# A masked prefix sum over eight batches: one ring of seven places, with tables of addresses, in place of two halves of five

## The chip, the cores and the metric

The kernel runs on 1 core of one Trainium2 chip. The metric is the time of one execution on the device in microseconds. The kernel before takes 88.33 us (median of 3 runs, 87.98 to 88.53).

## The reference

```python
def setup_inputs():
    B, S, D = 8, 8192, 512
    return {
        "x": np.random.randn(B, S, D).astype(np.float32),
        "lengths": np.random.randint(16, S, size=(B,)).astype(np.int64),
        "w": np.random.randn(D, D).astype(np.float32),
    }

def reference(x, lengths, w):
    ...
    mask = (pos < lengths[:, None, None]).astype(np.float32)
    cs = np.cumsum(x * mask, axis=1)
    mid_features = cs[b_idx, (lengths // 2).clip(0), :]
    return np.matmul(mid_features[:, None, :], w).squeeze(1).astype(np.float32)
```

Of each batch only the sum of its first n rows is needed, n = min(length // 2 + 1, length); eight sums of 512 columns are then multiplied by w. So the work is to read n rows for each batch, and n is known only on the chip. The draw is the same each time: n = 570, 2690, 256, 2057, 905, 3772, 3859, 571. In blocks of 512 rows (1 MB) that is 1, 5, 0, 4, 1, 7, 7, 1 whole blocks, 26 together, and a remainder for each batch.

## The kernel before

SyncE brings the whole blocks, ScalarE the remainders, TensorE sums the rows by products with columns of ones and zeros, VectorE makes those columns. Batches go in pairs, and each batch of a pair has its own half of the buffer with five places:

```python
    NP = 5
    xt = sb("xt", [P, 2, NP, G, D])
    ...
    nc.sync.dma_start(            # block 0 of batch 0, before the lengths are known
        out=xt[:, 0, 0], in_=xf[:BLK].rearrange("(p g) d -> p g d", g=G)
    ).then_inc(s_full[0][0], 16)
    ...
    # SyncE: the lengths of a pair are loaded into registers; a block is issued when its place is free
                def load(k):
                    sp.dma_start(
                        out=xt[:, q, k % NP],
                        in_=rows(sp, at, base, k * BLK, BLK).rearrange("(p g) d -> p g d", g=G),
                    ).then_inc(s_full[q][k % NP], 16)
                def load_block(k):
                    sp.wait_ge(s_sum, until[q][k % NP])
                    ...
```

TensorE goes over the batches, and in each over two rounds of five blocks; nested compares end a round early:

```python
                with pe.Fori(0, B // 2):
                    for q in range(2):
                        keep_busy()               # two idle products
                        take(pe, s_cur[q], 1)
                        take(pe, s_rem[q], 16 * (len(PARTS) + 1))
                        for j in range(G):        # the remainder
                            mm = add(j, cur[:, q, B + j * B:2 * B + j * B], rem[:, q, j])
                            ...
                        def add_block(k):
                            if k:
                                keep_busy()
                            take(pe, s_full[q][k], 16)
                            for j in range(G):
                                mm = add(j, cur[:, q, :B], xt[:, q, k, j])
                            mm.then_inc(s_sum, 1)
                        with pe.Fori(0, -(-NB // NP)):
                            whole_blocks(pe, n, NP, add_block)
                            pe.reg_alu(n, n, NP * BLK, ALU.subtract)
                            pe.reg_alu(n, n, 0, ALU.max)
                    ...
                # the signal: its end tells VectorE that the sums are complete
                pe.matmul(idle_ps[:1, :1], lhsT=idle[:, :1], rhs=idle[:, :1], start=True,
                          stop=True).then_inc(s_pe, 1)
```

The last block of the last batch is set aside: it lands in a tile of its own (`last`, two halves), and is added behind the signal, so that the copies of the sums run beside it. After the signal come two copies, small products into `t_ps`, two transposes, 32 output products and the copies and writes of the output. This is called the tail below.

Of the kernel before, what the change touches and what calls it, by code (L numbers as in the profile page):

```python
# [8 lines left out]
I32 = mybir.dt.int32  # L9
BF16 = mybir.dt.bfloat16  # L10
# [6 lines left out]
def kernel(  # L17
# [19 lines left out]

    nc = tc.nc
# [4 lines left out]
    NB = S // 2 // BLK  # L43
    NP = 5
# [6 lines left out]
    WT = B + G * B  # L51
# [16 lines left out]
    xt = sb("xt", [P, 2, NP, G, D])  # L68
# [6 lines left out]
    cut = sb("cut", [1, 1])  # L75
    blk_i = sb("blk_i", [1, B + 1], I32)
    ones = sb("ones", [1, P])
    cnt = sb("cnt", [P, B], I32)
    cap = sb("cap", [P, B, G], I32)
# [6 lines left out]
    idle = sb("idle", [P, D], BF16)  # L86
    table = sb("table", [P, B * (WT + 1)])
    cur = sb("cur", [P, 2, WT])
    zero = sb("zero", [1, P])
# [11 lines left out]

    s_full = [[sem(f"full{q}_{k}") for k in range(NP)] for q in range(2)]
    s_rem = [sem(f"rem{q}") for q in range(2)]
    s_cur = [sem(f"cur{q}") for q in range(2)]
    s_last = [sem(f"last{h}") for h in range(2)]
    s_zero = [sem(f"zero{q}") for q in range(2)]
    s_w, s_len1, s_go, s_out = sem("w"), sem("len1"), sem("go"), sem("out")
    s_pool, s_dve, s_pe = sem("pool"), sem("dve"), sem("pe")
    s_act, s_sum = sem("act"), sem("sum")
# [5 lines left out]
    class Pairs:  # L115


        def __init__(self, eng, ready, count):

            self.eng = eng  # L120
            self.raw = [eng.alloc_register(f"n_{eng.engine.name}_{i}") for i in range(4)]
            self.t = eng.alloc_register(f"t_{eng.engine.name}")
            self.at = eng.alloc_register(f"pair_{eng.engine.name}")
            eng.reg_mov(self.at, 0)
            eng.wait_ge(ready, count)
            eng.load(self.raw, lens1[:, :4])

        def rows(self, q):

            n = self.raw[2 * q]  # L130
            self.eng.reg_alu(self.t, n, 1, ALU.logical_shift_right)
            self.eng.reg_alu(self.t, self.t, 1, ALU.add)
            self.eng.reg_alu(n, self.t, n, ALU.min)
            return n

        def step(self):

            alu, top = self.eng.reg_alu, 2 * B - 4
            alu(self.at, self.at, 4, ALU.add)
            alu(self.at, self.at, top, ALU.min)  # L140
            self.eng.load(self.raw, lens1[:, ds(self.eng.snap(self.at, min_val=0, max_val=top), 4)])

    def whole_blocks(eng, n, most, body, k=0):
        if k < most:
            with eng.If_cmp(n, BLK * (k + 1), "IS_GE"):
                body(k)
                whole_blocks(eng, n, most, body, k + 1)


    DVE_SEL, DVE_N, DVE_BLK, DVE_MASK = 1, 5, 10, 31  # L150
    DVE_LAST = DVE_MASK + 6
# [4 lines left out]
    nc.sync.dma_start(  # L156
        out=xt[:, 0, 0], in_=xf[:BLK].rearrange("(p g) d -> p g d", g=G)
    ).then_inc(s_full[0][0], 16)
# [8 lines left out]
    @block.sync  # L167
    def _(sp):
        alu = sp.reg_alu
        base, at = sp.alloc_register("sp_base"), sp.alloc_register("sp_at")  # L170
        sp.reg_mov(base, 0)

        items = sp.alloc_register("sp_items")
        sp.reg_mov(items, 1)
        until = [[sp.alloc_register(f"until{q}_{k}") for k in range(NP)] for q in range(2)]
        for u in until[0] + until[1]:
            sp.reg_mov(u, 1)
        has_last, last_at = sp.alloc_register("has_last"), sp.alloc_register("last_at")
        sp.reg_mov(has_last, 0)
        sp.reg_mov(last_at, 0)  # L180

        least = sp.alloc_register("sp_least")
        sp.reg_mov(least, BLK)
        ns = Pairs(sp, s_len1, 16)
        sp.sem_inc(s_go, 1)
        with sp.Fori(0, B // 2):
            for q in range(2):
                n = ns.rows(q)
                alu(items, items, 1, ALU.add)
                if q == 0:  # L190
                    alu(n, n, least, ALU.max)
                    sp.reg_mov(least, 0)
                else:
                    with sp.If_cmp(ns.at, 2 * B - 4, "IS_GE"):
                        alu(has_last, n, 9, ALU.logical_shift_right)
                        alu(has_last, has_last, 1, ALU.min)
                        alu(last_at, has_last, 9, ALU.logical_shift_left)
                        alu(n, n, last_at, ALU.subtract)
                        alu(last_at, n, ~(BLK - 1), ALU.bitwise_and)
                        alu(last_at, last_at, base, ALU.add)  # L200

                def load(k):
                    sp.dma_start(
                        out=xt[:, q, k % NP],
                        in_=rows(sp, at, base, k * BLK, BLK).rearrange("(p g) d -> p g d", g=G),
                    ).then_inc(s_full[q][k % NP], 16)

                def load_block(k):
                    sp.wait_ge(s_sum, until[q][k % NP])
                    alu(items, items, 1, ALU.add)  # L210
                    sp.reg_mov(until[q][k % NP], items)
                    if (q, k) == (0, 0):

                        with sp.If_cmp(ns.at, 1, "IS_GE"):
                            load(k)
                    else:
                        load(k)

                whole_blocks(sp, n, NB, load_block)
                alu(base, base, S, ALU.add)  # L220
            ns.step()

        with sp.If_cmp(has_last, 1, "IS_GE"):
            from_rows = rows(sp, at, last_at, 0, BLK).rearrange("(p g) d -> p g d", g=G)
            for h in range(2):
                sp.dma_start(
                    out=last[:, 2 * h:2 * h + 2], in_=from_rows[:, 2 * h:2 * h + 2]
                ).then_inc(s_last[h], 16)
        sp.wait_ge(s_dve, DVE_LAST)
        sp.dma_start(out=out[:, :D // 2], in_=o_sb[0][:]).then_inc(s_out, 16)  # L230

    @block.scalar
    def _(act):
        alu = act.reg_alu
        base, at = act.alloc_register("act_base"), act.alloc_register("act_at")
        act.reg_mov(base, 0)
        items = act.alloc_register("act_items")
        act.reg_mov(items, 1)
        until = [act.alloc_register(f"until_rem{q}") for q in range(2)]
        for u in until:  # L240
            act.reg_mov(u, 1)
        least = act.alloc_register("act_least")
        act.reg_mov(least, 1)
        act.memzero(rem[:, 0]).then_inc(s_zero[0], 1)  # L244
        ns = Pairs(act, s_go, 1)
        t = ns.t
        with act.Fori(0, B // 2):
            for q in range(2):
                n = ns.rows(q)
                act.wait_ge(s_zero[q], 1)  # L250
                act.wait_ge(s_sum, until[q])
                alu(items, items, 1, ALU.add)
                alu(until[q], items, 1, ALU.max)
                alu(t, n, 9, ALU.logical_shift_right)
                if q == 0:
                    alu(t, t, least, ALU.max)
                    act.reg_mov(least, 0)
                alu(items, items, t, ALU.add)
# [32 lines left out]
            ns.step()  # L291

        act.wait_ge(s_pe, B + 5)
# [6 lines left out]
    @block.gpsimd  # L300
    def _(pool):
        pool.sem_inc(s_sum, 1)
        pool.iota(pid[:], pattern=[[0, 1]], base=0, channel_multiplier=1)
        pool.iota(thr_i[:], pattern=[[P, 2]], base=0, channel_multiplier=1)
        pool.iota(fold_i[:], pattern=[[-1, B]], base=128, channel_multiplier=1).then_inc(s_pool, 1)
        pool.memset(idle[:], 1.0).then_inc(s_pool, 1)
        pool.wait_ge(s_dve, DVE_BLK)
        pool.memset(rem[:, 1], 0.0).then_inc(s_zero[1], 1)  # L308

    @block.vector  # L310
    def _(dve):
        done = 0

        def step(do, *args, **kw):

            nonlocal done
            if done:
# [3 lines left out]

        step(dve.memset, zero[:], 0.0)
        assert done == DVE_SEL
        step(dve.memset, ones[:], 1.0)
# [6 lines left out]
        step(dve.tensor_copy, out=blk_i[:, :B], in_=n_f[:])  # L331
        step(dve.tensor_scalar, out=blk_i[:, :1], in0=n_f[:, :1], scalar1=BLK, scalar2=None, op0=ALU.max)
        step(dve.tensor_scalar, out=cut[:], in0=n_f[:, B - 1:], scalar1=BLK, scalar2=None, op0=ALU.is_ge)
        step(dve.tensor_copy, out=blk_i[:, B:], in_=cut[:])
        step(dve.scalar_tensor_tensor, out=blk_i[:, B - 1:B], in0=cut[:], scalar=float(-BLK),
             in1=n_f[:, B - 1:], op0=ALU.mult, op1=ALU.add)
# [36 lines left out]
        for b in range(B):  # L373
            if b == 0:
                dve.wait_ge(s_dve, done)
            if b >= 2:
                dve.wait_ge(s_pe, b + 1)
# [137 lines left out]
```

## Time and profile before

| | before |
|---|---|
| median, runs | 88.33 us, 3 runs |
| profiled run, its span | 88.74 us, 86.9 us |
| moved | 31.28 MB |
| first product of the last ring block ("the pickup") | 77.43 us |
| signal | 79.86 us |
| end of the last copy | 84.05 us |

The span is split by the last three rows: up to the pickup the kernel reads rows, from the pickup to the signal it finishes the sums, and behind the signal is the tail. Two stretches of reading matter, and the tail. The columns are: stretch, length, busy time and number of instructions of PE, PEld, DVE, ACT, POOL, then the clock of TensorE, the busy share of the DMA engines, and GB/s.

```profile
10.00:14.00 4.00, 0.18 (x4) 0.15 (x8) 0.00 (x0) 0.00 (x0) 0.00 (x0) 1.00 1.02 418
22.00:28.00 6.00, 6.00 (x44) 0.92 (x40) 0.00 (x0) 0.00 (x0) 0.00 (x0) 1.00 0.95 325
79.86:84.05 4.19, 3.01 (x77) 1.84 (x73) 1.91 (x6) 0.52 (x2) 0.00 (x0) 1.00 0.00 0
```

At 22 to 28 us there is the hole, (422 - 325) x 6 = 580 KB or 1.4 us of full rate; the tail takes 4.19 us, all of it at full clock.

### The profile page before, as it was taken

What the parts mean: (1) busy time and instruction counts of PE and PEld (TensorE: products, weight loads), DVE (VectorE), ACT (ScalarE), POOL (GpSimd) and SP (SyncE); (2) the same over time, 40 slices, a digit from 0 to 9 for tenths busy, and PEclk for the clock granted to TensorE, in tenths of its full rate; (3) what the DMA queues carried; (4) which work ended last, traced back from release to release, by engine and by line L of the source; (5) the groups of instructions that cost most, each with busy time, mean ns of one, the idle gap of its engine ahead of it and who ended that gap; (6) DMA issues with size and microseconds to landing.
All of it is one profiled execution on the core that took longest, in us unless ns stands there. A gap on an engine that the chain in (4) does not pass through costs nothing. (4 is left out here: it accounts for less than half of the span.)

```text
span 86.9 us, 1465 instructions
## 1 busy us (share of the span) xinstructions
PE 57.1 (66%) x391; PEld 10.9 (13%) x391; DVE 8.2 (9%) x45; ACT 3.7 (4%) x5; POOL 2.8 (3%) x9
## 2 busy tenths in 40 slices
PE   0912206999999998089967197655956774559730
PEld 0400001011111211002101001010110110103420
DVE  1776000000000100000000000000000000001420
ACT  2920000000000000000000000000000000000020
POOL 4340000000000000000000000000000000000000
PEclk9999999999999999957999956999999999999999
DMA  2799999999999999999999999999999999991000
GB/s 30 313 411 422 417 421 422 419 426 422 317 338 345 407 422 426 431 404 417 427 419 426 415 419 422 422 422 422 422 422 422 422 419 422 409 387 60 0 0 8
DMA packets 4837, 31.28 MB, mean 360 GB/s; under 512 B 674, under 2 KB 690, under 8 KB 1218
## 3 DMA queue, kind: packets, MB, share of 16 engines
q1 hardware_dynamic: 3906, 27.27, 76.5%
q10 hardware_dynamic: 928, 3.97, 11.9%
q8 instruction: 1, 0.02, 0.1%
q14 instruction: 2, 0.02, 0.0%
HBM read 31.23 MB, written 0.02 MB: 360 GB/s over the span
## 5 line engine op out<-in xcount | busy, mean ns | idle before, releaser
L395 PE MATMUL s_ps<-xt,cur 128*8 128x512 f32 x200 | 28.7, 647 | 15.3 <-PEq L113 15.2
L402 PE MATMUL idle_ps<-idle 128*128 128x512 bf16 x50 | 16.8, 422 | 3.6 <-DVE table L319 3.5
L395 PE MATMUL s_ps<-rem,cur 128*8 128x512 f32 x64 | 9.8, 688 | 4.7 <-PEq L113 4.7
L395 PEld LDWEIGHTS s_ps<-xt,cur 128*8 128x8 f32 x200 | 4.0, 90 | 30.5 <-issue 30.4
L378 DVE COPY cur<-table 128x40 f32<-128x40 f32 x8 | 1.4, 184 | 53.4 <-PE s_ps L395 53.4
L402 PEld LDWEIGHTS idle_ps<-idle 128*128 128x128 bf16 x50 | 2.9, 99 | 26.8 <-issue 26.8
L295 ACT COPY o_sb<-o_ps 8x128 f32<-8x128 f32 x2 | 0.5, 258 | 78.6 <-PE o_ps L477 78.6
L413 PE MATMUL s_ps<-zero 1*128 1x512 f32 x2 | 2.1, 1131 | 2.3 <-DVE n_i L319 2.3
L319 DVE COPY s_sb<-s_ps 128x256 f32<-128x256 f32 x2 | 0.8, 424 | 17.3 <-PE idle_ps L450 17.3
L395 PEld LDWEIGHTS s_ps<-rem,cur 128*8 128x8 f32 x64 | 1.0, 88 | 9.3 <-issue 9.3
L244 ACT ACTIVATE rem<-rem 128x2048 uint32<-128x2048 uint32 x1 | 1.9, 1910 | 0.0
L308 POOL MEMSET rem<- 128x2048 f32 x1 | 1.8, 1805 | 1.7 <-DVE blk_i L319 1.7
L477 PE MATMUL o_ps<-wt,t_sb 128*8 128x128 f32 x32 | 1.1, 273 | 0.4 <-DVE t_sb L319 0.4
L244 ACT ACT_TABLE_LOAD x1 | 1.3, 1283 | 1.5 <-PEq L499 1.5
L406 PE MATMUL t_ps<-last,cur 128*8 128x128 f32 x32 | 1.3, 272 | 0.0
L477 PEld LDWEIGHTS o_ps<-wt,t_sb 128*8 128x8 f32 x32 | 0.8, 89 | 0.7 <-issue 0.7
L406 PE MATMUL t_ps<-s_sb,fold 128*8 128x128 f32 x8 | 0.8, 274 | 0.1
L416 PEld LDWEIGHTS n_ps<-n_f,ones 1*128 1x128 f32 x2 | 0.7, 332 | 1.0 <-DVE cut L319 0.5
L413 PEld LDWEIGHTS s_ps<-zero 1*128 1x128 f32 x2 | 0.5, 304 | 2.3 <-DVE n_i L319 2.3
L406 PEld LDWEIGHTS t_ps<-last,cur 128*8 128x8 f32 x32 | 0.8, 88 | 0.1
L319 DVE COPY o_sb<-o_ps 8x128 f32<-8x128 f32 x2 | 0.6, 281 | 1.0 <-PE o_ps L477 1.0
L319 DVE STREAM_TRANSPOSE t_sb<-t_ps 128x64 f32<-128x64 f32 x2 | 0.5, 250 | 1.0 <-PE t_ps L406 0.9
(43 smaller groups left out, 7.1 us busy)
## 6 DMA issues: line engine op xcount, KB each, us to landing
xt<-in_x_dram SPq DMA_DIRECT2D x25, 1024.0 KB, 12.7
rem<-in_x_dram ACTq DMA_DIRECT2D x3, 512.0 KB, 7.0
wt<-in_w_dram ACTq DMA_DIRECT2D x1, 1024.0 KB, 6.5
last<-in_x_dram SPq DMA_DIRECT2D x2, 512.0 KB, 10.2
rem<-in_x_dram ACTq DMA_DIRECT2D x3, 256.0 KB, 6.3
rem<-in_x_dram ACTq DMA_DIRECT2D x3, 128.0 KB, 7.1
rem<-in_x_dram ACTq DMA_DIRECT2D x3, 32.0 KB, 5.8
rem<-in_x_dram ACTq DMA_DIRECT2D x1, 64.0 KB, 6.1
```

The lines of the kernel that those rows point to most:

```text
L244: act.memzero(rem[:, 0]).then_inc(s_zero[0], 1)
L295: copy = act.copy(out=o_sb[1][:, j * P:(j + 1) * P], in_=o_ps[64 + 32 * j:64 + 32 * j + B, :P])
L308: pool.memset(rem[:, 1], 0.0).then_inc(s_zero[1], 1)
L319: do(*args, **kw).then_inc(s_dve, 1)
L378: dve.tensor_copy(out=cur[:, b % 2], in_=table[:, b * WT:(b + 1) * WT]).then_inc(s_cur[b % 2], 1)
L395: return pe.matmul(s_ps[32 * j:32 * j + B], lhsT=weights, rhs=rows, start=False, stop=False, skip_group_check=True, tile_position=(0, 32 * j))
L402: pe.matmul(idle_ps[:], lhsT=idle[:, :P], rhs=idle[:], start=True, stop=True)
L406: return pe.matmul(t_ps[32 * j:32 * j + B, :P], lhsT=weights, rhs=row[:, P * j:P * (j + 1)], start=False, stop=False, skip_group_check=Tru ...
L413: pe.matmul(s_ps[:], lhsT=zero[:], rhs=zero[:, :1].to_broadcast((1, D)), start=True, stop=False, skip_group_check=True)
L416: pe.matmul(n_ps[:, :B], lhsT=ones[:], rhs=n_f[:], start=True, stop=True).then_inc(s_pe, 1)
L477: mm = pe.matmul(o_ps[32 * j:32 * j + B, :P], lhsT=t_sb[:, kc, :B], rhs=wt[:, kc, j * P:(j + 1) * P], start=(kc == 0), stop=(kc == KC - 1) ...
```

## The change

The intent: the hole at 22 us comes from a buffer split by batch, where a long batch fills its half while the other half stands empty. One ring of seven places serves the blocks of all batches in order. For that each engine has to know which batch and which rows the i-th block of the ring is. VectorE works that out at the start: a table of the first row of every ring item (`addr`) and a table of the weight columns of every item (`wtab`). SyncE loads seven addresses at a time into registers; VectorE copies each item's weights into its place's columns when the place is freed, and then hands the place to SyncE. The first blocks of batches 0 and 1 are fetched blind, with known addresses, before anything is computed. SyncE, VectorE and TensorE walk a fixed number of rounds of seven items: ceil(63 / 7) = 9, enough for the longest lengths that can be drawn. The remainders are added by pairs in the first four rounds. Cut to its core:

```diff
-    NP = 5
+    BLIND = 2
+    NS = 7
+    ROUNDS = -(-(B * S // 2 // BLK - 1) // NS)
+    ITEMS = ROUNDS * NS
-    xt = sb("xt", [P, 2, NP, G, D])
+    xt = sb("xt", [P, NS, G, D])
+    def nested(eng, n, most, body, k=0):
         if k < most:
-            with eng.If_cmp(n, BLK * (k + 1), "IS_GE"):
+            with eng.If_cmp(n, k + 1, "IS_GE"):
                 body(k)
-                whole_blocks(eng, n, most, body, k + 1)
+                nested(eng, n, most, body, k + 1)
+    def less(eng, n, by):
+        eng.reg_alu(n, n, by, ALU.subtract)
+        eng.reg_alu(n, n, 0, ALU.max)
+    for b in range(BLIND):
+        nc.sync.dma_start(
+            out=xt[:, b], in_=xf[b * S:b * S + BLK].rearrange("(p g) d -> p g d", g=G)
+        ).then_inc(s_full[b], 16)
 # SyncE
+        sp.wait_ge(s_dve, DVE_ADDR)
+        sp.load(facts, meta[:])
+        sp.reg_mov(left, facts[0])
+        with sp.Fori(0, ROUNDS):
+            sp.load(at, addr[:, ds(sp.snap(off, min_val=0, max_val=ITEMS - NS), NS)])
+            def load(k):
+                take(sp, s_free[k], 1)
+                sp.dma_start(
+                    out=xt[:, k], in_=xf[ds(sp.snap(at[k]), BLK)].rearrange("(p g) d -> p g d", g=G)
+                ).then_inc(s_full[k], 16)
+            ...
+            nested(sp, left, NS, load_item)
+            less(sp, left, NS)
+            ...
+        with sp.If_cmp(facts[1], 1, "IS_GE"):     # the block set aside
+            ...
 # GpSimd
-        pool.wait_ge(s_dve, DVE_BLK)
-        pool.memset(rem[:, 1], 0.0).then_inc(s_zero[1], 1)
+        pool.wait_ge(s_dve, DVE_N)
+        pool.memset(rem[:, 1], 0.0).then_inc(s_rfree[1], 1)
 # VectorE: ... tables, 28 steps to the first addresses (DVE_ADDR), 51 to TensorE's start (DVE_MASK)
+        step(dve.tensor_scalar, out=blocks[:], in0=cnt[:], scalar1=9, scalar2=None,
+             op0=ALU.logical_shift_right)
+        ...
+        with dve.Fori(1, ROUNDS):
+            less(dve, left, NS)
+            ...
+            def weights(k):
+                take(dve, s_done[k], 1)
+                dve.tensor_copy(out=cur[:, k], in_=wtab[...]).then_inc(s_free[k], 1)
+            nested(dve, left, NS, weights)
 # TensorE
+        with pe.Fori(0, ROUNDS):
+            with pe.If_cmp(rest_rounds, 1, "IS_GE"):
+                for q in range(2):
+                    take(pe, s_rem[q], 16 * (len(PARTS) + 1))
+                    ...
+            def add_item(k):
+                keep_busy()
+                take(pe, s_full[k], 16)
+                for j in range(G):
+                    mm = add(j, cur[:, k], xt[:, k, j])
+                mm.then_inc(s_done[k], 1)
+            nested(pe, left, NS, add_item)
+            less(pe, left, NS)
+            less(pe, rest_rounds, 1)
+        tell()                                    # the signal
```

## The prediction

> **What bounds the kernel now.** I read the page's slices first, then the chain that ended last, then stretches of the span with their transfer rates, then the issues of transfers and the tensor engine's register work.
>
> ```profile
> PEclk9999999999999999957999956999999999999999
> DMA  2799999999999999999999999999999999991000
> GB/s 30 313 411 422 417 421 422 419 426 422 317 338 345 407 422 426 431 404 417 427 419 426 415 419 422 422 422 422 422 422 422 422 419 422 409 387 60 0 0 8
> PE 5%; DVE 2%; issue 0%
> ```
>
> From slice 3 to slice 35 the DMA engines move some 420 GB/s with every engine busy. 31.28 MB at that rate is 74 us of an 86.9 us span, so the kernel is bound by reading the rows, and the chain that ended last, 7% of the span, is only the tail behind the last rows. The one hole in the middle is slices 10 to 13. The same in stretches (columns: stretch, length, busy time and count of PE, PEld, DVE, ACT, POOL, then the PE clock, DMA share, GB/s):
>
> ```profile
> 16.00:22.00 6.00, 6.00 (x36) 0.74 (x28) 0.18 (x1) 0.00 (x0) 0.00 (x0) 1.00 1.01 422
> 22.00:23.00 1.00, 1.00 (x10) 0.23 (x10) 0.00 (x0) 0.00 (x0) 0.00 (x0) 1.00 0.92 262
> 23.00:25.00 2.00, 2.00 (x18) 0.23 (x10) 0.00 (x0) 0.00 (x0) 0.00 (x0) 1.00 0.96 365
> 25.00:28.00 3.00, 3.00 (x24) 0.46 (x20) 0.00 (x0) 0.00 (x0) 0.00 (x0) 1.00 0.94 320
> 34.00:76.00 42.00, 27.71 (x171) 4.13 (x170) 0.55 (x3) 0.00 (x0) 0.00 (x0) 0.92 1.01 421
> ```
>
> Against 422 GB/s the hole lost 160 x 1 + 57 x 2 + 102 x 3 = 580 KB, or 1.4 us. Its cause stands in the time line of SyncE's issues:
>
> ```profile
> 4.73 4.70 SPq L203 DMA_DIRECT2D xt<-in_x_dram  x5
> 21.12 45.52 SPq L203 DMA_DIRECT2D xt<-in_x_dram  x19
> ```
>
> Nothing is issued between 9.4 and 21.1 us: batch 1 fills all five places of its half (this draw's whole blocks per batch are 1, 5, 0, 4, 1, 7, 7, 1), and the next batch that has any uses the same half. TensorE starts only at 13.8, when the first remainder has landed, so a place comes free just as the queue runs dry at 22.
>
> [...]
>
> ```profile
> 33.17:36.58 3.41, 1.29 (x10) 0.11 (x2) 0.00 (x0) 0.00 (x0) 0.00 (x0) 1.00 1.00 423
> 36.58:39.99 3.41, 2.76 (x10) 0.28 (x10) 0.00 (x0) 0.00 (x0) 0.00 (x0) 0.50 1.01 408
> 46.83:50.24 3.41, 1.11 (x14) 0.24 (x10) 0.00 (x0) 0.00 (x0) 0.00 (x0) 1.00 1.01 418
> 50.24:53.65 3.41, 2.81 (x18) 0.28 (x10) 0.00 (x0) 0.00 (x0) 0.00 (x0) 0.50 1.04 425
> ```
>
> A stretch of 3.41 us with 1.1 to 1.3 us of matmuls is followed by one at clock 0.50; one with 2.1 us is not. [...] The trace of TensorE's sequencer differs: 64 to 72 ns where the program falls through, 200 to 220 ns where it jumps; I use those. [...] in the chain of table steps one 1x8 or 128x8 operation follows another every 0.19 us, a small memset every 0.13.
>
> **The change part by part.**
>
> *Places.* Seven places for all batches in place of two halves of five. After the two blind blocks SyncE can issue five more, so seven blocks (one more than now) are queued before any place must come free. The first place comes free at about the same time: TensorE now needs the remainders of batches 0 and 1 first (the second lands at 16.1 now; perhaps 14.5, its queue being shorter), 3.8 us of cold matmuls for both, then 1.0 for the idle pair and 1.0 for block 0, so about 20.5, plus VectorE's copy and the issue: 21.0. But with 1 MB more queued (2.5 us at 422 GB/s) the queue runs dry at 24.5 to 25 rather than 22. The new block is there in time, and TensorE then frees one every 1.5 us while one lands every 2.5. I expect most of the hole to close: **-1.2 us**.
>
> *Tables.* SyncE's first computed issue waits for 28 VectorE steps. Eight memsets from 1.0 to 2.3 us, three steps on the lengths to 2.9, four memsets, the broadcast of counts through TensorE until about 3.8, then thirteen steps of 0.19: 6.3 us. Two register loads (0.5 us for one here now) and some branches: first issue at 8.5 to 9, against 4.73 now. Three MB (weights, two blind blocks) plus the first remainders keep the engines busy until 10.5 to 12, since now the third such MB lands at 12.4. With about 1.2 us from issue to first packet (a reading of the first transfers), 10 us is just in time. The other 23 steps to TensorE's start end at about 11.8, before the remainders land. **0 us**, at worst +1.
>
> *Steady state.* Same bytes, same transfers of 1 MB; one 128x8 copy and one more hand-over per block on VectorE, hidden behind a depth of six blocks. **0 us**.
>
> *The end.* Here is what I think decides. The chain, and the register work at the end of the last two batches (TensorE's sequencer):
>
> ```profile
> 77.43 1.04 PE s_ps L395 x8
> 78.47 0.54 PE idle_ps L402 x2
> 79.01 0.97 PE s_ps L395 x8
> 79.98 0.10 PE idle_ps L450
> L145 PEldq COMPARE_BRANCH  x2: 201/206/210, 78.4 to 79.0; - x2
> L444 PEldq FUSED_REGOPS  x2: 53/53/53, 78.7 to 79.3; - x2
> L442 PEldq COMPARE_BRANCH  x2: 69/138/207, 78.8 to 79.4; - x2
> ```
>
> Now the last block is picked up at 77.3 and the signal matmul (L450), which releases the tail, starts at 79.86: 2.55 us for its four products, an idle pair and the last remainder. In the new kernel that remainder comes earlier, but the loop has ceil(63/7) = 9 rounds whatever the lengths are. This draw has 25 items in the ring (26 whole blocks, the last set aside): 3 full rounds, one of four, and **five empty rounds**, which TensorE's sequencer walks through after the last block, ahead of the signal. The rows show an empty turn of the present inner loop: 78.4, 78.7, 78.8, and again at 79.0, so a jumped compare costs 0.26, the register work 0.11, the jump back 0.26. An empty round has two jumped compares (remainders, items), one register group of four operations (0.15) and the jump back: 0.53 + 0.15 + 0.26 = 0.94. From pickup: 0.15 to the first compare, 0.68 for the rest of the fourth round, 5 x 0.94 less the 0.13 that the last saves = 4.57. Sum 5.4 us against 2.55: **+2.85 us**. The set-aside block lands at 78.6 and 79.8 now and hides none of it.
>
> *The clock.* Of these 5.4 us the matmuls fill 1, so a gap of over 4 us opens. [...] part of the tail (signal, 24 small products, 32 output products: 0.16 + 0.85 + 1.1 us warm, twice that cold) runs at half clock. At most +2, half of it on average: **+1.0 us**.
>
> Sum: 88.33 - 1.2 + 0 + 2.85 + 1.0 = **91.0 us**.
>
> **Rivals.** (A) *The intended gain.* The empty rounds cost little (the sequencer runs ahead of the matmuls), the hole closes, and the last remainder's 1.5 us leave the tail: then the set-aside block bounds the tail, which ends about 1.2 us earlier, plus 1.3 from the hole: 86. For it: at 77.5 the next compare does start while the products still run. Against it: they run 1 us, and the walk takes five. (B) *A new hole at the start.* The tables come late, the queue runs dry at 10 us and restarts with slow first packets, like now at 22: up to +1 to +1.5, so 92 to 92.5. For it: 28 steps and two loads are worked out with a margin of only a microsecond. Against: the remainders fill in. (C) *The hole stays*, since PE waits for two remainders and three hand-overs: 92.2. The rate stays low for 3 us after issues resumed, which speaks for it a little. (D) *The clock stays up* in the tail: 90.
>
> **Range and chances.** The main terms are the walk (2.85 +- 0.7), the clock (0 to 2), the hole (-1.4 to 0) and the start (0 to 1). Together some +-1.9 us for 8 in 10: 89.0 to 92.7. Two per cent up is 90.1; the sum lies 0.9 above it. Faster by over 2% (below 86.6) needs rival A whole: 0.04. Within 2%: 0.28. Slower: 0.68.
>
> **What would show it.** In the new profile: the rate at 20 to 30 us near 420 (hole closed) and the last block picked up at about 76; SyncE's first computed issue at 8.5 to 9 with no dip at 9 to 13; five repeats of two compares at TensorE's sequencer, 0.9 us each, between the last block and the signal matmul, which starts over 5 us after the pickup; a clock record of 0.50 in the tail; VectorE's wait for the signal in the chain. The prediction is wrong if the signal comes within 3 us of the pickup, or if the rate at the start drops.

## The result

The changed kernel takes **93.35 us** (median of 4 runs, 92.72 to 93.50), the kernel before 88.43 us (4 runs, 87.98 to 89.27) beside it. The ratio is 1.053 (95% interval 1.044 to 1.063): slower. A ratio, here and below, is the mean time of one kernel's runs over that of the other's (in the experiments without the profiled run), so not quite the ratio of the medians that are quoted. Executions over 1.5% slower than the fastest of the same kernel are left out of the means.

In the changed kernel's page, the slices of clock and rate and the shares of the chain that ended last:

```profile
PEclk9999999999999999999999999999999999997597
GB/s 29 340 416 426 369 288 413 437 419 416 434 408 423 416 423 430 415 395 426 412 423 430 416 416 430 408 426 416 419 423 426 419 419 407 177 2 0 0 0 7
PE 5%; issue 5%; DVE 1%
```

The hole in slices 10 to 13 (counted from 0) is gone. A dip has appeared in slices 4 and 5. The last transfer of rows lands just before 80 us in both kernels, but a longer stretch without any follows here, the clock falls to half in a part of it (its record is 0.50 from 82.9 to 86.3 us), and "issue" (time in which the engine waits for nothing that the profile shows), which had 0% of the chain, has 5%. The same stretches as before, with the tail last (signal to last copy):

```profile
10.00:14.00 4.00, 0.00 (x0) 0.00 (x0) 3.56 (x11) 0.00 (x0) 0.00 (x0) 1.00 0.90 314
11.00:12.00 1.00, 0.00 (x0) 0.00 (x0) 0.98 (x1) 0.00 (x0) 0.00 (x0) 1.00 0.76 115
22.00:28.00 6.00, 5.84 (x43) 0.92 (x40) 0.68 (x4) 0.00 (x0) 0.00 (x0) 1.00 1.01 418
82.83:87.77 4.94, 3.83 (x73) 2.67 (x73) 1.91 (x6) 0.52 (x2) 0.00 (x0) 0.65 0.00 0
```

At 22 to 28 us the rate rose from 325 to 418, which is what the ring was made for. At 10 to 14 us it fell from 418 to 314, a loss of 416 KB or 1.0 us, most of it in one microsecond. The tail ran at a mean clock of 0.65. The end of the chain, in order of time (start, duration, engine, tile, line, count):

```profile
77.61 1.05 PE s_ps L430 x8
78.65 4.18 issue
82.83 0.16 PE idle_ps L447
82.99 2.45 PE t_ps L436 x40
```

and what TensorE's sequencer did in the 4.18 us of "issue" (columns: line, operation, count, shortest, median and longest in ns, then the time of the first and of the last):

```profile
L136 PEldq COMPARE_BRANCH  x6: 201/201/207, 77.7 to 82.3; - x6
L461 PEldq COMPARE_BRANCH  x5: 201/201/201, 78.3 to 82.0; - x5
L141 PEldq FUSED_REGOPS  x6: 78/78/78, 77.9 to 82.5; - x6
```

L136 is the compare "is there a block k", L461 "are there remainders", L141 the two `less`. The first compare is the one that ends the fourth round; then the sequencer goes round five times with nothing to do, 0.92 us each ((82.3 - 77.7) / 5), and only then issues the signal (L447). Where the 3.8 us between the two spans (86.9 and 90.7 us) are:

| stretch | before | after | difference |
|---|---|---|---|
| start to pickup of the last ring block | 77.43 | 77.61 | +0.2 |
| pickup to signal | 2.43 | 5.22 | +2.8 |
| signal to end of the last copy | 4.19 | 4.94 | +0.75 |

So reading gained nothing, though its hole is closed; the walk through empty rounds stands between the last data and the signal; and the tail behind it runs partly at half clock.

### The profile page after: what moved, and what is told of

The parts are those of the page before. It is cut to its first block, busy times and chain, and to the rows that moved or that the text cites. A ratio compares the mean times of both kernels' runs of the same rounds, so it can differ in the third digit from the quotient of the medians.

```text
span 90.7 us, 1568 instructions
## 1 busy us (share of the span) xinstructions
PE 53.3 (59%) x387; PEld 11.6 (13%) x391; DVE 17.5 (19%) x86; ACT 3.7 (4%) x5; POOL 3.0 (3%) x11
## 5 line engine op out<-in xcount | busy, mean ns | idle before, releaser
L430 PE MATMUL s_ps<-xt,cur 128*8 128x512 f32 x200 | 26.1, 593 | 16.5 <-PEq L131 16.4
L430 PE MATMUL s_ps<-rem,cur_rem 128*8 128x512 f32 x64 | 9.3, 707 | 9.1 <-PEq L131 9.1
L443 PE MATMUL idle_ps<-idle 128*128 128x512 bf16 x46 | 14.2, 384 | 0.6 <-issue 0.6
L404 DVE COPY cur<-wtab 128x8 f32 x18 | 3.1, 171 | 36.3 <-DVEq L131 36.3
L430 PEld LDWEIGHTS s_ps<-rem,cur_rem 128*8 128x8 f32 x64 | 1.8, 95 | 15.8 <-issue 15.7
L447 PE MATMUL idle_ps<-idle 128*1 128x1 bf16 x1 | 0.2, 163 | 4.2 <-issue 4.2
L436 PE MATMUL t_ps<-last,e_last 128*8 128x128 f32 x32 | 2.3, 414 | 0.0
L397 DVE COPY cur_rem<-table 128x32 f32 x6 | 1.1, 182 | 5.8 <-DVEq L131 5.8
L436 PEld LDWEIGHTS t_ps<-last,e_last 128*8 128x8 f32 x32 | 1.3, 121 | 0.2
L289 DVE TENSOR_TENSOR wtab<-since 128x504 f32<-128x504 f32 x1 | 1.1, 1066 | 0.0
L289 DVE TENSOR_TENSOR part_a<-since,step_a 1x49 f32<-1x49 f32 (+1 forms) x2 | 1.1, 529 | 0.1
```

Of the source, the lines that this page charges most:

```text
L289: do(*args, **kw).then_inc(s_dve, 1)
L397: dve.tensor_copy(out=cur_rem[:, q], in_=rests[:, ds(dve.snap(at, min_val=1, max_val=B // 2 - 1), 1), q].rearrange("p o w -> p (o w)"),).t ...
L404: dve.tensor_copy(out=cur[:, k], in_=wtab[:, ds(dve.snap(at, min_val=1, max_val=ROUNDS - 1), 1), k].rearrange("p o b -> p (o b)"),).then_i ...
L430: return pe.matmul(s_ps[32 * j:32 * j + B], lhsT=weights, rhs=rows, start=False, stop=False, skip_group_check=True, tile_position=(0, 32 * j))
L436: return pe.matmul(t_ps[32 * j:32 * j + B, :P], lhsT=weights, rhs=row[:, P * j:P * (j + 1)], start=False, stop=False, skip_group_check=Tru ...
L443: pe.matmul(idle_ps[:], lhsT=idle[:, :P], rhs=idle[:], start=True, stop=True)
```

## The experiments

The theory after reading the two traces had four parts, each with a rival:

- *Walk*: the empty rounds of TensorE's loop hold the signal back. Rival: the signal waits for something else (a block, VectorE's own rounds), and cutting rounds moves nothing.
- *Clock*: the half clock from 82.9 us comes from that wait ("cold" is half clock here and below, "warm" is full clock), and the tail, 4.94 us in place of 4.19, pays for it. Rival: the slower tail comes from the new kernel's tail itself.
- *Start*: late tables open the new hole at 11 us, which takes back what the ring gains. Rival: the ring gained nothing, and both holes are hidden by the total of bytes.
- *Places*: the seventh place is what closes the hole at 22 us. Rival: the common ring alone does it, or the blind blocks.

Ten kernels ran, in three calls, each with runs of the kernel before on the same chip. In the second call (from e5 to e8) the runs of the kernel before are the first call's, made some ten minutes earlier, and one new one. The changed kernel itself wasn't run again beside the experiments.

### Four rounds only (e1_four_rounds)

TensorE walks only the rounds that this draw needs. The result is right for this draw only.

```diff
-        with pe.Fori(0, ROUNDS):
+        with pe.Fori(0, 4):
```

> TensorE's loop has 4 rounds in place of 9: right for this draw alone, whose 25 items fill 4. Theory (the walk through five empty rounds is 4.6 us of the loss, and the idle gap it makes costs 0.7 to 1.9 us more in the tail through the half clock): the signal matmul starts about 1.2 us after the last block is picked up (5.3 now), the tail runs at full clock, and the set-aside block, landing at about 80.0 us of the span, now bounds the tail. Time 87.7 +- 0.5 us, that is 5 to 6 us under the changed kernel and about 0.99 of the kernel before. Rival (the loss sits in the start or the transfers, and the walk hides behind the set-aside block): 92 us or more.

Measured: 88.19 us (87.61 to 88.79, 4 runs), ratio to before 0.9997 (0.990 to 1.009). The chain's end:

```profile
77.57 1.04 PE s_ps L430 x8
78.61 0.07 PE idle_ps L447
```

The signal comes 1.04 us behind the pickup in place of 5.22, and the tail behind it (78.61 to 82.76, 4.15 us) is warm again. The five empty rounds and their cold tail are therefore the whole of the loss, and VectorE's and SyncE's own empty rounds, which are still there, cost nothing that this kernel's chain shows. The set-aside block, which was expected to bound the tail, doesn't stand in the chain. What is left is ring, tables and weights together: the same time as before within about 1%. In the profiled runs this kernel's span was 1.2 us below before's, but two of its four runs were 0.6 to 0.9 us longer than the profiled one, and there is no trace of those.

### Warm walk (e2_warm_walk)

The empty rounds stay, but each has an idle pair in it, so that only the clock changes.

```diff
                     mm.then_inc(s_rdone[q], 1)
+            with pe.Else():
+                keep_busy()
```

> The walk stays, but in each empty round TensorE gets one idle pair (0.5 us of matmuls per 0.91 us round). Theory (part of the loss is the half clock that the idle gap brings): signal still 5.3 us (up to 5.6) after the pickup of the last block; no clock record of 0.50 in the tail; from the signal to the last copy 4.2 us as in the kernel before, in place of 4.9 in the profiled run. Time 92.1 us (91.7 to 92.6), 1.0 to 1.5 below the changed kernel, its runs at a mean clock near 1. Rival (the clock costs nothing): unchanged, 93.3.

Measured: 91.47 us (91.33 to 92.42, 4 runs), ratio 1.039 (1.029 to 1.049). The first idle pair of the walk and the signal, in the chain that ended last:

```profile
78.00 0.60 PE idle_ps L443 x2
...
82.47 0.12 PE idle_ps L447
```

The pickup is at 76.80, so the signal comes 5.7 us behind it (the idle pairs add 0.5), and the tail takes 4.06 us (82.47 to 86.53), all at full clock. So the slower tail was the clock's. The time lies a little below the expected range. Against the changed kernel it is 1.4% or 1.3 us by the ratios, whose intervals overlap a little, and 1.9 us by the medians, of different rounds. In this profiled run the pickup was 0.8 us earlier too, which the edit doesn't explain (start and tables are unchanged), so the clock's share can't be told from it better than "around 1 us".

### Known rows (e3_known_rows)

SyncE issues the five ring blocks behind the blind ones at once, with this draw's row numbers written in, and doesn't wait for the tables in round 0 (round 0 of its loop then issues nothing; that part of the edit isn't shown). Right for this draw only.

```diff
+        known = [S + k * BLK for k in (1, 2, 3, 4)] + [3 * S]
+        for k, row in zip(range(BLIND, NS), known):
+            take(sp, s_free[k], 1)
+            sp.dma_start(
+                out=xt[:, k], in_=xf[row:row + BLK].rearrange("(p g) d -> p g d", g=G)
+            ).then_inc(s_full[k], 16)
         sp.wait_ge(s_dve, DVE_ADDR)
```

> SyncE issues the first five blocks of the ring at once, with this draw's rows written into the program (wrong for other draws), so nothing at the start waits for the tables; the rest is as in the changed kernel. Theory (the late tables cost a hole at 11 to 13 us that ate most of what the ring won): the rate at 10 to 14 us stays near 420 GB/s, the last block is picked up 0.7 to 1.0 us earlier (76.5 to 76.9), time 92.4 (92.0 to 92.8). Rival (the engine that is furthest behind sets the last landing, and it lost less than the mean in that hole): a gain of 0.3 or less, 93.0 to 93.4. Second rival (more early blocks delay the remainders' landing and with it TensorE's start, so that the hole comes back at 22 to 28): no gain.

Measured: 92.20 us (92.05 to 92.41, 4 runs), ratio 1.044 (1.036 to 1.052). The rates, and the pickup:

```profile
11.00:12.00 1.00, 0.00 (x0) 0.00 (x0) 0.98 (x1) 0.00 (x0) 0.00 (x0) 1.00 1.05 426
22.00:28.00 6.00, 5.84 (x43) 0.92 (x40) 0.69 (x4) 0.00 (x0) 0.00 (x0) 1.00 1.00 411
76.59 1.04 PE s_ps L432 x8
```

With the hole at the start gone and the one at 22 us still closed, the pickup is 1.0 us earlier (76.59 against 77.61): the size worked out from the rate. The pickup alone wouldn't settle it, since in the warm walk it was 0.8 us earlier with the start unchanged. The bytes do better: over the first 76 us the mean rate is 406 GB/s here, against 400 in the changed kernel and 401 in the warm walk, so some 0.4 to 0.5 MB more were read, or 0.9 to 1.1 us of full rate. So the wait for the tables took back about 1 us, by one trace of each; in time it is 0.8 us by the ratios, whose intervals overlap, and 1.15 us by the medians, of different rounds. Its walk still took 5.2 us, and its tail ran at half clock almost to its end (mean clock 0.57), 81.81 to 87.38, 5.57 us against 4.19 warm.

### GpSimd's memset later (e4_pool_later)

One reason for the late tables was visible in the time line of the changed kernel (start, duration, engine, line, operation, tiles, and what ended the idle time before it):

```profile
2.90 1.80 POOL L278 MEMSET rem<- 128x2048 f32 x1 [0.82 <-DVE n_f L289]
3.79 0.94 DVE L289 TENSOR_SCALAR blocks<-cnt 128x8 int32<-128x8 int32 x1
```

A shift of 128x8 numbers takes 0.94 us and ends at 4.73, just when GpSimd's memset ends at 4.70; the operations of 128x8 numbers next to it, at 3.59 and 4.77, take 0.17 us each. That the shift waits for the memset is the estimate from these times. The experiment lets the memset wait for the address table instead.

```diff
-        pool.wait_ge(s_dve, DVE_N)
+        pool.wait_ge(s_dve, DVE_ADDR)
         pool.memset(rem[:, 1], 0.0).then_inc(s_rfree[1], 1)
```

> GpSimd's memset of the second remainder place waits for step 28 of the tables in place of step 11. Theory (VectorE's shift of the counts took 0.94 us in place of 0.16 because it stood still until that memset ended): the shift takes 0.16 us, SyncE's first computed issue comes at 9.2 to 9.3 us in place of 10.04, and the hole at 11 to 13 us shrinks from 0.95 us to 0.2 to 0.5; time 92.7 (92.3 to 93.1). Rival (the shift is slow for another reason): still 0.9 us, no change of time.

Measured: 92.77 us (92.64 to 92.96, 4 runs), ratio 1.050 (1.042 to 1.058). The shift and SyncE's issues of this kernel, and SyncE's issues of the changed kernel, in that order:

```profile
3.78 0.17 DVE L289 TENSOR_SCALAR blocks<-cnt 128x8 int32<-128x8 int32 x1
9.27 52.41 SPq L179 DMA_DIRECT2D xt<-in_x_dram  x23
```

```profile
10.04 51.90 SPq L179 DMA_DIRECT2D xt<-in_x_dram  x23
```

The shift takes 0.17 us with the memset out of its way, in place of 0.94; how the memset held it up, no run shows. The first computed issue moves by the 0.77 us that the shift lost, and the rate at 10 to 14 us rises from 314 to 367, but a hole remains (238 and 352 GB/s in 10 to 11 and 11 to 12 us), and the gain in time is within the intervals. Other delays in front of that issue are two register loads on SyncE, in the changed kernel 0.88 and 0.95 us.

### Empty rounds first (e5_empty_first)

A version that is made to be right for any lengths (only this draw was run): TensorE walks the same number of rounds, but the empty ones come first, while it waits for the tables anyway. A register starts at the number of items (at least 22, for the remainders) and grows by seven each round; a round has work when it has reached 57.

```diff
+        gate = pe.alloc_register("pe_gate")
+        pe.reg_alu(gate, left, NS * (B // 2 - 1) + 1, ALU.max)
         with pe.Fori(0, ROUNDS):
-            with pe.If_cmp(rest_rounds, 1, "IS_GE"):
-                ...
-            nested(pe, left, NS, add_item)
+            with pe.If_cmp(gate, NS * (ROUNDS - 1) + 1, "IS_GE"):
+                pe.wait_ge(s_dve, DVE_MASK)
+                with pe.If_cmp(rest_rounds, 1, "IS_GE"):
+                    ...
+                nested(pe, left, NS, add_item)
+                ...
+            pe.reg_alu(gate, gate, NS, ALU.add)
```

> A general cure for the walk: the same nine rounds, but the empty ones come first, while TensorE waits for its first rows anyway (a register starts at the number of items and gains 7 a round; a round runs only from 57 on), and its loop count is read after the address tables, not after all tables. All else as in the changed kernel. Theory (only the place of the walk, behind the last block, costs): five empty turns of 0.65 us between 8 and 13 us, hidden; signal about 1.2 us after the last pickup; time as with four rounds, 88.0 (87.4 to 88.6), ratio to the kernel before 0.985 to 1.005. Rival (the longer loop body or the later start costs elsewhere): above 89.

Measured: 87.84 us (87.55 to 88.20, 6 runs), ratio 0.994 (0.988 to 1.000). The walk is gone from the end, as in the kernel with four rounds, without knowing the draw. The first computed issue was still at 10.05 us, one issue took 1.5 us in the profiled run, and the loss at the start was larger there (293 GB/s at 10 to 14, 382 at 14 to 22 us), so the pickup was at 77.87.

### Empty rounds first and an earlier start (e6_both)

The kernel above, with the later memset, one register load in place of two ahead of the first issue, and what the set-aside block needs worked out and loaded later.

```diff
-        sp.load(facts, meta[:])
-        sp.reg_mov(left, facts[0])
+        sp.load([left] + at, plan[:, :1 + NS])
         with sp.Fori(0, ROUNDS):
-            sp.load(at, addr[:, ds(sp.snap(off, min_val=0, max_val=ITEMS - NS), NS)])
             ...
             sp.wait_ge(s_dve, DVE_ALL)
+            sp.load(at, plan[:, ds(sp.snap(off, min_val=0, max_val=ITEMS - NS) + 1, NS)])
+        sp.load(facts, ends[:])
         with sp.If_cmp(facts[0], 1, "IS_GE"):
```

> As the run with the empty rounds first, and also: GpSimd's memset waits for the address tables; the number of items and the first addresses lie in one tile that SyncE reads with one load in place of two; the two facts on the set-aside block are made after the tables and read at the end. Theory (the hole at the start is the rest of the loss, worth the 1.0 us that the known rows gained): first computed issue at 7.3 to 8.3 us in place of 10.04, rate near 420 from 9 to 14 us, last pickup at 76.5 to 76.9, time 87.0 (86.6 to 87.6), ratio to the kernel before 0.975 to 0.99. Rival (the hole only moves, to where the places come free, 22 to 28 us): as without these, 88.0.

Measured: 87.58 us (87.30 to 88.03, 6 runs), ratio 0.991 (0.985 to 0.997); 87.0 was expected. Two things were not foreseen. SyncE's issues:

```profile
7.64 53.38 SPq L178 DMA_DIRECT2D xt<-in_x_dram  x23
73.94 0.87 SPq L201 DMA_DIRECT2D last<-in_x_dram  x2
```

The first issue came 2.4 us earlier than in the changed kernel, yet a hole remained: 286 GB/s at 10 to 12 us, 352 at 12 to 14. The blind blocks landed at 8.2 and 10.75, so the new transfers had been issued behind them before the queue ran dry, and still the rate fell. (The profiled run was the slowest of the six, so the others may have lost less.) And SyncE has empty rounds of its own, each with a register load of 0.93 to 1.50 us: only behind them is the set-aside block issued, at 73.94. It lands at 80.1, and in this kernel, where the signal no longer comes late, that bounds the tail.

### Six places (e7_six_places)

The same kernel with one place less, which makes eleven rounds of six, to test *places*.

```diff
-    NS = 7
+    NS = 6
```

> As the run before it, with six places in place of seven (11 rounds of 6, the walk still first; the kernel before has six blocks queued before the first place must come free, too). Theory (the seventh place is what closes the hole at 22 to 28 us): the queue runs dry at about 22, the rate at 22 to 28 us falls to 320 to 380, time 0.6 to 1.4 us above the run with seven: 88.0 (87.5 to 88.7). Rival (the ring as such, not its size, closes the hole): no dip, the same time as with seven.

Measured: 94.71 us (93.97 to 95.21, 4 runs), ratio 1.074 (1.065 to 1.084); 88.0 was expected. The hole at 22 us came back, as the part *places* says (320 GB/s at 22 to 28 us), while this run has none at the start (412 at 10 to 14 us); but it is the smaller loss:

```profile
22.00:24.00 2.00, 1.84 (x15) 0.30 (x12) 0.34 (x2) 0.00 (x0) 0.00 (x0) 1.00 0.81 274
79.77 1.26 SPq L201 DMA_DIRECT2D last<-in_x_dram  x2
```

SyncE has six empty rounds here, one more than with seven places, each with a load of 1.27 us. They delay the set-aside block to 79.77; TensorE waits for it until 83.9. So this run doesn't measure the seventh place. It shows the same fault as the walk, on another engine.

### The walk put into the kernel before (e8_before_walk)

Five empty turns ahead of the signal of the kernel *before*, with nothing else changed.

```diff
+                none = pe.alloc_register("pe_none")
+                pe.reg_mov(none, 0)
+                with pe.Fori(0, 5):
+                    for _ in range(2):
+                        with pe.If_cmp(none, 1, "IS_GE"):
+                            keep_busy()
+                    for _ in range(2):
+                        pe.reg_alu(none, none, 7, ALU.subtract)
+                        pe.reg_alu(none, none, 0, ALU.max)
                 pe.matmul(idle_ps[:1, :1], ...).then_inc(s_pe, 1)     # the signal
```

> The kernel before, with five empty turns (two jumped compares, four register operations, a jump back) put ahead of its signal matmul and nothing else changed. Theory (register work behind the last block goes straight to the time, whatever the kernel): the signal starts 6.5 to 7.1 us after the last pickup in place of 2.45, because the walk starts when the last remainder is issued; a half clock in the tail; time 88.6 + 4.4 + 1.0 = 94.0 (93.0 to 95.0). Rival (the walk is partly hidden by the set-aside block or the matmuls): under 92.

Measured: 94.81 us (94.36 to 95.28, 4 runs), ratio 1.073 (1.063 to 1.082).

```profile
77.32 1.04 PE s_ps L395 x8
78.36 0.54 PE idle_ps L402 x2
78.90 0.97 PE s_ps L395 x8
79.87 4.59 issue
84.47 0.16 PE idle_ps L460
```

From pickup to signal it takes 7.15 us in place of 2.43: the walk alone adds 4.7. The tail behind it, 84.47 to 90.05, takes 5.58 us in place of 4.19, at half clock: 1.4 more. Together 6.1, and by the ratio 0.0725 x 88.4 = 6.4 us: walk and clock alone cost the old kernel more than the changed kernel lost. The change also took the last remainder and an idle pair out of this stretch, 1.5 us of the chain above (78.36 to 79.87).

This run shows one thing more, which the comparison of the two first traces hides. The code that reads the rows is unchanged here, yet it moved 407 GB/s at 22 to 28 us, against 325 in the first trace of the kernel before, and 374 at 8 to 14 us, against 421; the pickup was at 77.32, against 77.43. So the kernel before doesn't lose its rate at 22 us in each execution, and "325 became 418" compares one execution with one. What holds over all traces: with seven places none of eight has less than 411 GB/s at 22 to 28 us.

### No loads in SyncE's empty rounds (e9_no_idle_loads), and six places again (e10_six_no_idle_loads)

```diff
-            sp.wait_ge(s_dve, DVE_ALL)
-            sp.load(at, plan[:, ds(... + 1, NS)])
+            with sp.If_cmp(left, 1, "IS_GE"):
+                sp.wait_ge(s_dve, DVE_ALL)
+                sp.load(at, plan[:, ds(... + 1, NS)])
```

The second kernel has `NS = 6` besides. They ran in the same rounds.

> As e6_both (empty rounds first on TensorE, one plan tile, later memset), and SyncE reads the next round's addresses only where items are left, so that its own empty rounds hold no register load (1.0 to 1.5 us each there). Theory (in e6_both SyncE's walk issued the set-aside block at 73.9, so late that the queue ran dry behind the last block of the ring and the set-aside block bound the tail): set-aside block issued before 68 us, rate at 76 to 78 us back near 400, its second half landed 2.5 us after the last pickup instead of 3.35, time 86.8 (86.2 to 87.3), ratio to the kernel before 0.97 to 0.985. Rival (the late issue cost nothing): 87.6 as e6_both.

> The same with six places. In e7_six_places the whole loss but 0.7 us stood in the set-aside block, issued at 79.8 behind six loads of 1.27 us; the dip at 22 to 28 us (274, 356, 328 GB/s) did come. Theory: without those loads 94.7 falls to 87.4 (86.9 to 88.2), that is 0.3 to 1.2 above the run with seven places: the seventh place closes the hole at 22 to 28 us and that is what it is worth. Rival (six places are slower for another reason, such as the two more rounds): 89 or more. Second rival (the place is worth nothing because the hole only moves): the same time as with seven.

Measured: with seven places 87.00 us (86.72 to 87.73, 6 runs), ratio 0.986 (0.983 to 0.989), the best version, 1.4% better than the kernel before (clear of its interval) and made for any lengths. With six places 88.01 us (87.81 to 88.84, 5 runs), ratio 0.999 (0.995 to 1.003). In the kernel with seven places the set-aside block is issued in time:

```profile
66.89 0.86 SPq L202 DMA_DIRECT2D last<-in_x_dram  x2
```

The seventh place is worth about 1.1 us (1.2% between the two ratios, 1.0 us between the medians, with whatever the two more rounds of the loops with six places cost counted in), close to the 1.4 us of the hole. The hole at the start stays in the profiled run of this version (320 GB/s at 10 to 14 us, pickup at 77.73), which was the slowest of its six runs (87.73). That the version gains 1.4% where the kernel with four rounds gained nothing isn't fully explained: the two ran in different rounds on different chips, and there is no trace of the faster runs.

## Why the prediction was right and wrong

The direction and the main mechanism were right; the time was 2.3 us too low, and 93.35 lies 0.65 above the range. By its own steps:

- **The end, +2.85 us: right.** Measured +2.8 (5.22 against 2.43; the prediction had 5.4 against 2.55, with the pickup read at 77.3 in place of 77.43). An empty round was put at 0.94 us; it takes 0.92, and there are five of them. Cutting them, and putting them into the old kernel, both move the time as this asks.
- **The clock, +1.0 us: right in kind.** The step was the estimate from the two half-clock stretches in the trace of before (from 36.58 and 50.24 us, 3.41 us each). The tail of the profiled run took 0.75 us more, partly at half clock; at half clock throughout or nearly so, as in two experiments and in the old kernel with the walk, 1.4 more. How much is paid differs from run to run: in the changed kernel's trace the clock fell at 82.9 us, just behind the signal, and rose again at 86.3, while in e3 it had fallen at 79.7, before the signal, and rose at 86.6. The three unprofiled runs of the changed kernel have a lower mean clock (0.905 to 0.913 against 0.976) and are 0.5 to 0.8 us longer; a wholly cold tail fits that, but there is no trace of them, and the mean clock alone doesn't tell (with four rounds it was 0.913 beside a warm tail).
- **Places, -1.2 us, and tables, "0 us, at worst +1": here it failed.** Taken together they were to move the pickup of the last block 1.2 us forward; it moved 0.2 us back. The places did their part: 325 became 418 GB/s at 22 to 28 us in the two first traces, and six places in the best version cost 1.1 us. It was the step on the tables that failed. The first computed issue came at 10.04 us and not at 8.5 to 9: the shift beside GpSimd's memset (0.94 against the 0.19 that each step was given, +0.75) and two register loads of 0.88 and 0.95 against some 0.5 each (+0.8). That is rival B, "a new hole at the start": its size was well put (+1 to +1.5, measured 1.0), but the sum took the mid-line of 0. Writing in the addresses removed the hole and moved the pickup by 1.0 us. By the prediction's own list of signs ("or if the rate at the start drops") it was wrong here. The second half of the step, that an issue by 10 us is just in time, isn't borne out either: in e6 and e9 the first computed issue came at 7.6 us, ahead of the 8.5 to 9 that was forecast, and the rate at 10 to 14 us was still 319 and 320 GB/s. Against the 418 of before the loss there is 416 KB with the issue at 10.04 us, 204 at 9.27 (e4), 24 at 8.02 (e7) and some 395 at 7.6 (e6, e9), so the time of the issue alone doesn't set it, and what does is not shown.
- **A small rest.** -1.2 and +1.0 would still be -0.2 where +0.2 was measured. By the mean rates the changed kernel had even read a little more by 77 us. The sixteen parts of the last block landed over 1.8 us, against 1.5 before, and the last part sets the pickup; that this is the cause was only argued from the two traces.
- **The steady state, 0: right.** 419 to 421 GB/s in both from 28 to 76 us, with one copy more for each block on VectorE.

In sum, for the profiled runs: predicted -1.2 + 0 + 2.85 + 1.0 = +2.65; measured +0.2 + 2.8 + 0.75 = +3.75 us. The difference of 1.1 is the places and tables (1.4) less 0.25 at the clock. The rest up to the difference of the medians, 4.9 us, is that the profiled run of the changed kernel was its fastest and that of the kernel before was slower than its median.

What stays open: why transfers issued at 7.64 us, before the queue ran dry, left a hole at 10 to 14 us, while known rows issued at 2.3 us removed it and the run with six places, issued at 8.02 us, had none; where the kernel before loses its rate in runs without a trace; and why the pickup of two kernels with the same start differs by 0.8 us from run to run.

## What to carry to other kernels

A loop whose count is fixed for the worst case walks its empty rounds behind the last data, in front of whatever waits for its end; on TensorE that was 0.92 us a round, and at half clock the tail behind it took 0.75 to 1.4 us more. Put the empty rounds first, where the engine waits anyway, and look at every engine that has the loop, also the one that issues transfers: its empty rounds can delay the last transfer, above all with a register load in each (0.93 to 1.50 us in e6, which issued its last transfer at 73.94 us; e9, without them, at 66.89). A deeper queue can close the hole that it was made for (325 became 418 GB/s in the two first traces), but work put in front of the first issue can open another one as large (1.0 us here): count that chain with the loads and with what other engines do beside it, and book the two together.

## Small costs in the traces

- On TensorE's sequencer the traces of before and after show mostly 64 to 73 ns for a compare-and-branch that falls through and 201 to 223 ns for one that jumps; an empty round of two jumped compares, register work and the jump back took 0.92 us.
- On SyncE the trace of before has register loads of four words in 497 ns the first time and 297 to 311 ns later. The runs show no fixed cost for a word: in the changed kernel three words took 877 ns and seven 934 to 1488, in later rounds mostly 1467 or more.
- A shift of 128x8 numbers beside a GpSimd memset of 128x2048 took 0.94 us, and 0.17 with the memset later (e4).
- In the trace of before, the clock was at half from 36.58 and from 50.24 us, 3.41 us each time. The 3.41 us just ahead were busy with products for 1.29 and 1.11 us; the stretches of that length from 53.65 and from 57.06 us were busy for 2.13 and 2.05 us, and full clock followed. A tail behind 4.2 to 4.6 us of walking took 4.94 to 5.58 us in place of 4.19.
